# A hybrid decoder step on one core: the sample's state update split anew between ScalarE and VectorE, its loads fetched earlier, and a scan step regrouped

## The chip, the core and the metric

The kernel runs on one core of one Trainium2 chip. Its time is the device time of one execution in microseconds (us). Before the change three runs gave 2443.49, 2448.03 and 2448.24 us, a median of 2448.03.

## What is computed

The reference is one layer of a decoder trunk for a prompt of 1024 tokens and a sample group of 8 tokens, which share all weights. After a modulated RMS norm one input projection feeds attention and a Mamba-2 scan; both are merged, projected, and followed by a second norm and an MLP. The part that the change touches is the scan, with its gate, and the second norm:

```python
def _ssd_mixer(z, xbc, dt_raw, conv_buf, h0, conv_w, conv_b, dt_bias, a_log, d_skip, norm_g):
    xbc, new_buf = _causal_conv(xbc, conv_buf, conv_w, conv_b)
    xs = xbc[..., :D_INNER].reshape(b, L, SSD_HEADS, SSD_HEAD_DIM)
...
    y, h = _ssd(xs, dt, A, Bm, Cm, h0)
    y = y + d_skip.astype(jnp.float32)[:, None] * xs.astype(jnp.float32)
    y = _gated_rmsnorm(y.reshape(b, L, D_INNER).astype(z.dtype), z, norm_g)
    return y, new_buf, h
```

The scan has 32 heads of 64 channels, 8 groups that share their B and C, and a state of 128. For the prompt it goes over 8 chunks of 128 tokens. For a sample, which has one token, it is one update of each state: `h = h * decay + (x * dt) * B`, and then `y = sum(h * C)` over the state.

## The kernel before

**Dense work and side work.** All large products go through the class `Dense`. A job is one block of 128 output features: its weights are loaded by SyncE (L81, tile `wraw`), rounded by ScalarE to a high part (L94, `whi`), and split by GpSimd into the low part (L95, `wlo`). For each of three token chunks (384, 384 and 264 columns) and each of eight slices of the contraction, TensorE makes three matmuls (L140 to L142), 24 for a chunk, into one of 3 PSUM banks called `mm`. Then the job's own evacuation empties the bank. Other work is written as Python generators, the sides. Between two chunks of a dense job a clock advances and the sides are resumed; `yield from rest(n)` lets n such steps pass. They use 5 other PSUM banks, called `ps`.

**Order.** TensorE's order is the order in which the program is written, so the steps of the sides set it. The other engines' orders are made by a scheduler from the dependencies, and they keep it: each takes its instructions one after the other. SyncE issues every DMA, in one queue.

**A group of the scan.** For each of the 8 groups (`gi`) dense jobs compute the gate stream z (L785 tanh on ScalarE, L786 on VectorE) and then four blocks of the stream that goes through the convolution. The first two of these I call x and x', and x.c0 is the first token chunk of x. Their evacuation is L819 on ScalarE, three multiply-adds on VectorE (L823), which free the bank, then a tanh (L832) and one more VectorE step (L833). While they run, three sides work on the group whose convolution is done:

- `decode` updates the sample states. `load(bh)` fetches, for a pair of samples, B and C spread over all partitions (L867, tile `bc`, 256 KB) and for two feature tiles the state (L872, tile `hst`). Each feature tile and sample then has: ScalarE's product of B with x·dt (L887, `tmp`); VectorE's `hst * decay + tmp` (L888); VectorE's sum of `hst * C` (L890). The state is stored (L892), and L893 adds the result to x. A group has 16 updates, the kernel 128.
- `chunks` goes over the 8 chunks. `load(c)` fetches the running sums of the decay (L906, tile `ar`, 256 KB). `prep(c)` transposes x and B and multiplies B with C on TensorE (L917 to L920), empties that bank (L925, L928 and L930 on VectorE, L927 on ScalarE), and turns `ar` into decays (four instructions of L932 and one of L934 on ScalarE, L935 on GpSimd). `state(c)` makes the new state (L941 on TensorE, L944 decay on GpSimd, L947 add on VectorE). `out(c)` makes the output (L956 from the old state, L960 from the chunk; L964, L965 and L967 on VectorE).
- `finish_` multiplies with the gate (L978 on GpSimd), stores (L979), squares (L980 on ScalarE, L981 on VectorE) and sums the squares over the channels (`sums`, on TensorE L284, read by L987).

Some of the groups also have gate jobs among their dense work, whose tanh is stored at L1153.

**The second norm.** Late in the program `norm2(ci)` waits until all eight output projections of a token chunk are done. L284 sums the squares over the channels, a Newton iteration on VectorE takes the reciprocal root, L1407 spreads it over the partitions, and eight feature tiles are normalised (L1410 to L1416) as the input of the MLP's first projection. ScalarE and VectorE square and sum beforehand (L1357, L1358).

## Time and profile before

| | |
|---|---|
| three runs | 2443.49, 2448.03, 2448.24 us; median 2448.03 |
| profiled execution, its own time | 2446.0 us |
| span of its trace | 2444.1 us, mean granted TensorE clock 0.982 |
| busy | TensorE 95%, VectorE 49%, ScalarE 35%, GpSimd 28% |

The profile names engines PE (TensorE), PEld (its weight loads), DVE (VectorE), ACT (ScalarE), POOL (GpSimd) and SP (SyncE). `L888` is a line of the kernel; `hst<-hst,dsel,tmp` is what an instruction writes and reads. An idle time belongs to the engine just before the instruction named, with what ended it behind an arrow. The profiled execution lies 2.0 us below the median of the runs.

### The profile page before, as it was taken

The page shows a single profiled execution, that of the slowest core. Times are in us where ns is not written, and L with a number is a line of the kernel's source. Part 1 is how long each engine was busy: PE and PEld are TensorE (multiplying, and loading weights), DVE is VectorE, ACT ScalarE, POOL GpSimd, SP SyncE. Part 2 cuts the span into 40 slices and gives each one's busy share as a digit, 9 for nine tenths or more (in the row PEclk, how much of TensorE's full clock was granted, in tenths as well). Part 3 has the DMA queues.
Part 4 walks back from the last instruction along what each step waited for, and adds up shares of the span by engine and source line. Part 5 has one row for each costly group of instructions (what it writes and reads, how often), then busy time and mean ns, then how long its engine had stood idle before and what let it go on. Part 6 is the DMA issues. An engine that isn't in the chain of part 4 may idle for free.

```text
span 2444.1 us, 40657 instructions
## 1 busy us (share of the span) xinstructions
PE 2333.1 (95%) x15171; PEld 2227.6 (91%) x15171; DVE 1191.2 (49%) x3224; ACT 861.5 (35%) x2138; POOL 686.8 (28%) x615
## 2 busy tenths in 40 slices
PE   6989999999999989999999899999999999999997
PEld 4868888989888988989999899999999999999997
DVE  3533334575666657476654644546433333333336
ACT  4433433454444444354533331233321221221232
POOL 1102122233333333343443323441222212222230
PEclk8989999999999999999999999999999999999999
DMA  8345434353443434344345532440544444411111
GB/s 304 111 148 158 149 90 101 87 145 107 114 110 98 121 89 118 94 116 123 101 136 153 150 109 87 120 152 22 168 143 149 157 149 152 136 48 44 57 40 70
DMA packets 359588, 288.61 MB, mean 118 GB/s; under 512 B 24030, under 2 KB 350237, under 8 KB 353614
## 3 DMA queue, kind: packets, MB, share of 16 engines
q1 hardware_dynamic: 359390, 286.01, 39.7%
q8 instruction: 120, 1.97, 0.3%
q14 instruction: 78, 0.64, 0.1%
HBM read 243.77 MB, written 88.74 MB: 136 GB/s over the span
## 4 chain that ended last, share of the span: by engine, by line
PE 70%; DMA 12%; DVE 8%; ACT 3%; issue 3%; POOL 3%; SPq 1%; DVEq 0%; ACTq 0%; POOLq 0%
PE mm L140 21%; PE mm L141 21%; PE mm L142 21%; DMA ar<-ac_d 7%; DVE ck L823 2%; ACT ar L932 1%; PE ps L571 1%; DMA wraw<-w_in 1%; POOL wlo L95 1%; DMA bc<-bc_d 1%; DVE hst L888 1%; PE ps L545 1%; POOL ar L935 1%; DVE tmp L890 1%; PE ps L562 1%
## 5 line engine op out<-in xcount | busy, mean ns | idle before, releaser
L140 PE MATMUL mm<-hh,whi 128*128 128x384 f32 (+4 forms) x2808 | 927.1, 330 | 29.8 <-DVE ck L823 27.0
L141 PE MATMUL mm<-hl,whi 128*128 128x384 f32 (+4 forms) x2808 | 902.3, 321 | 0.8 <-DMA xT_d<-xT 0.4
L142 PE MATMUL mm<-hh,wlo 128*128 128x384 f32 (+4 forms) x2808 | 902.1, 321 | 0.0
L95 POOL TENSOR_TENSOR wlo<-wraw,whi 128x512 fp32r<-128x512 f32 (+2 forms) x332 | 425.0, 1285 | 1204.4 <-ACT whi L94 1163.7
L140 PEld LDWEIGHTS mm<-hh,whi 128*128 128x128 f32 (+1 forms) x2808 | 532.5, 190 | 45.0 <-issue 27.7
L141 PEld LDWEIGHTS mm<-hl,whi 128*128 128x128 f32 (+1 forms) x2808 | 531.6, 189 | 5.5 <-DVE hl L417 2.2
L142 PEld LDWEIGHTS mm<-hh,wlo 128*128 128x128 f32 (+1 forms) x2808 | 530.8, 189 | 1.2
L94 ACT CAST whi<-wraw 128x512 fp32r<-128x512 f32 (+2 forms) x332 | 201.4, 610 | 460.0 <-PE mm L141 393.1
L1342 DVE SCALAR_TENSOR_TENSOR acc<-mm,mod,acc 128x384 f32<-128x384 f32 (+1 forms) x216 | 123.5, 572 | 229.4 <-PE mm L142 229.3
L141 PE MATMUL mm<-dl,whi 128*128 128x384 f32 (+1 forms) x696 | 223.3, 321 | 0.0
L142 PE MATMUL mm<-dh,wlo 128*128 128x384 f32 (+1 forms) x696 | 222.3, 319 | 0.0
L140 PE MATMUL mm<-dh,whi 128*128 128x384 f32 (+1 forms) x696 | 222.3, 319 | 0.0
L823 DVE SCALAR_TENSOR_TENSOR ck<-mm,cwT,ck 128x384 f32<-128x384 f32 (+4 forms) x288 | 162.9, 567 | 58.2 <-ACT ck L819 54.2
L1436 DVE TENSOR_TENSOR r<-r 128x384 f32<-128x384 f32 (+1 forms) x96 | 69.5, 724 | 186.0 <-ACT r L1435 186.0
L935 POOL TENSOR_TENSOR ar<-ar,cb 128x512 f32<-128x512 f32 x64 | 84.4, 1323 | 180.4 <-DVE cb L930 170.9
L932 ACT ACTIVATE ar<-ar,acs 128x128 f32<-128x128 f32 x256 | 85.9, 393 | 129.4 <-DMA ar<-ac_d 128.5
L140 PEld LDWEIGHTS mm<-dh,whi 128*128 128x128 f32 x696 | 131.0, 188 | 0.0
L141 PEld LDWEIGHTS mm<-dl,whi 128*128 128x128 f32 x696 | 130.9, 188 | 0.0
L142 PEld LDWEIGHTS mm<-dh,wlo 128*128 128x128 f32 x696 | 130.8, 188 | 0.0
L888 DVE SCALAR_TENSOR_TENSOR hst<-hst,dsel,tmp 128x128 f32<-128x128 f32 x128 | 66.3, 539 | 69.0 <-ACT tmp L887 58.8
L1435 ACT ACTIVATE r<-mm 128x384 f32<-128x384 f32 (+1 forms) x96 | 43.8, 456 | 154.6 <-PE mm L142 154.1
L832 ACT ACTIVATE th<-ck 128x384 f32<-128x384 f32 (+1 forms) x96 | 47.2, 492 | 108.0 <-DVE ck L823 108.0
(358 smaller groups left out, 3371.5 us busy)
## 6 DMA issues: line engine op xcount, KB each, us to landing
wraw<-w_in SPq DMA_DIRECT2D x164, 256.0 KB
kv_g_sample<-cache_kv_g SPq DMA_DIRECT2D x144, 256.0 KB
wada<-w_ada SPq DMA_DIRECT2D x24, 1024.0 KB
ar<-ac_d SPq DMA_DIRECT2D x64, 256.0 KB
wraw<-w_up SPq DMA_DIRECT2D x64, 256.0 KB
wraw<-w_down SPq DMA_DIRECT2D x58, 256.0 KB
hst<-state_ssm SPq DMA_DIRECT2D x64, 128.0 KB
bc<-bc_d SPq DMA_DIRECT2D x32, 256.0 KB
```

Of the source, the lines that this page charges most:

```text
L94: A.copy(hi, raw)
L95: P.tensor_tensor(lo, raw, hi, op=OP.subtract)
L140: T.matmul(ps[:n, :m], wh, a, start=(k == 0), stop=False)
L141: T.matmul(ps[:n, :m], wh, b, start=False, stop=False)
L142: T.matmul(ps[:n, :m], wl, a, start=False, stop=(k == nk - 1))
L823: V.scalar_tensor_tensor(acc[:, o:n], ps[:, x0 + o - d:x0 + n - d], w[k], acc[:, o:n], op0=OP.mult, op1=OP.add)
L832: A.activation(th[:, :nt], acc[:, :nt], AF.Tanh)
L888: V.scalar_tensor_tensor(hst[:, i, :], hst[:, i, :], ds[:, 8 + 2 * bh + i:9 + 2 * bh + i], tmp, op0=OP.mult, op1=OP.add)
L932: A.activation(ar[:, h, :], ar[:, h, :], AF.Relu, bias=acs[:, c, 4 * gi + h:4 * gi + h + 1], scale=-1.0)
L935: P.tensor_tensor(ar, ar, cb[:, None, :].to_broadcast([128, 4, 128]), op=OP.mult)
L1342: V.scalar_tensor_tensor(x[:, t0:t0 + n], ps[:, :n], gate[:, 0:1], x[:, t0:t0 + n], op0=OP.mult, op1=OP.add)
L1436: V.tensor_tensor(r[:, :nt], r[:, :nt], r[:, :nt], op=OP.mult)
```

## The change

Five things change.

1. In `decode`, ScalarE multiplies the state by its decay in place, and VectorE adds B times x·dt to it; before, ScalarE made the product with B and VectorE did the decay and the sum. VectorE's multiply-add now waits for ScalarE's decay, which needs nothing that VectorE makes in that step.
2. `bc` has 3 buffers instead of 2, `hst` 6 instead of 4, and loads are issued for two pairs ahead of the loop and a third in its first step. A step of the side is now one feature tile, with one `rest(1)`, instead of a pair with `rest(2)`.
3. In `chunks`, `prep(c + 3)` and `load(c + 4)` stand in the step of `state(c)`; `out(c)` follows a step later.
4. In `finish_`, the gate's products with their stores and the squares are two steps.
5. In `norm2`, two steps pass before the reciprocal root instead of one.

```diff
--- before.py
+++ after.py
@@ -863,19 +863,20 @@
             def load(bh):
                 if bh > 3:
                     return
-                bc = sd.tile([128, 2, 2, 128], F32, name="bc", tag="bc", bufs=2)
+                bc = sd.tile([128, 2, 2, 128], F32, name="bc", tag="bc", bufs=3)
                 dma(bc, dap(bc_d, gi * 2048 + bh * 256, [[0, 128], [1024, 2], [128, 2], [1, 128]]))
                 hs_ = []
                 for t in range(2):
                     r0 = bh * 2 * 262144 + (4 * gi + 2 * t) * 8192
-                    hst = sd.tile([128, 2, 128], F32, name="hst", tag="hst", bufs=4)
+                    hst = sd.tile([128, 2, 128], F32, name="hst", tag="hst", bufs=6)
                     dma(hst, dap(ws, r0, [[128, 128], [262144, 2], [1, 128]]))
                     hs_.append((r0, hst))
                 got[bh] = bc, hs_
             load(0)
-            yield from rest(2)
+            load(1)
+            yield from rest(3)
             for bh in range(4):
-                load(bh + 1)
+                load(bh + 2)
                 bc, hs_ = got[bh]
                 for t, (r0, hst) in enumerate(hs_):
                     ds = dsel[:, 2 * gi + t, :]
@@ -884,14 +885,14 @@
                     V.tensor_tensor(dx[:, :2], xcol, ds[:, 2 * bh:2 * bh + 2], op=OP.mult)
                     for i in range(2):
                         tmp = sd.tile([128, 128], F32, name="tmp", tag="tmp", bufs=3)
-                        A.mul(tmp, bc[:, 0, i, :], dx[:, i:i + 1])
-                        V.scalar_tensor_tensor(hst[:, i, :], hst[:, i, :], ds[:, 8 + 2 * bh + i:9 + 2 * bh + i],
-                                               tmp, op0=OP.mult, op1=OP.add)
+                        A.mul(hst[:, i, :], hst[:, i, :], ds[:, 8 + 2 * bh + i:9 + 2 * bh + i])
+                        V.scalar_tensor_tensor(hst[:, i, :], bc[:, 0, i, :], dx[:, i:i + 1], hst[:, i, :],
+                                               op0=OP.mult, op1=OP.add)
                         V.tensor_tensor_reduce(tmp, hst[:, i, :], bc[:, 1, i, :], 1.0, 0.0,
                                                OP.mult, OP.add, dx[:, 4 + i:5 + i])
                     dma(dap(wso, r0, [[128, 128], [262144, 2], [1, 128]]), hst)
                     V.scalar_tensor_tensor(xcol, xcol, ds[:, 16:17], dx[:, 4:6], op0=OP.mult, op1=OP.add)
-                yield from rest(2)
+                    yield from rest(1)
             tl['dec'] = 1
 
         A_, S_ = {}, {}
@@ -977,6 +978,8 @@
             for t in range(2):
                 P.tensor_tensor(X[t][ci][:, :nt], X[t][ci][:, :nt], Z[t][ci][:, :nt], op=OP.mult)
                 dma(y_d[2 * gi + t, :, t0:t0 + nt], X[t][ci][:, :nt])
+            yield from rest(1)
+            for t in range(2):
                 A.activation(sq[t][:, :nt], X[t][ci][:, :nt], AF.Square)
             V.tensor_tensor(sq[0][:, :nt], sq[0][:, :nt], sq[1][:, :nt], op=OP.add)
             if nt < 384:
@@ -1002,11 +1005,11 @@
             yield from rest(1)
             for c in range(8):
                 state(c)
-                yield from rest(1)
-                out(c)
                 if c + 3 < 8:
                     prep(c + 3)
                 load(c + 4)
+                yield from rest(1)
+                out(c)
                 tl['c'] = c + 1
                 if c in (2, 5, 7):
                     live[c // 6] -= 2
@@ -1026,7 +1029,7 @@
                 while tl['c'] < min(8, 3 * ci + 3) or tl['nz'] < 6 or (ci == 2 and not tl['dec']):
                     yield 'wait'
                 yield from rest(1)
-                gate(ci)
+                yield from gate(ci)
                 yield from rest(2)
                 sums(ci)
                 yield
@@ -1399,7 +1402,7 @@
             yield 'wait'
         if nt < 384:
             V.memset(ssq[ci][:, nt:], 0.0)
-        yield from rest(1)
+        yield from rest(2)
         r = rstd_cols(ssq[ci], 1.0 / D, EPS, n2)
         yield from rest(1)
         ps = ps_()
```

Since the diff adds lines, L887 becomes L888, L888 becomes L889, L906 becomes L907, L932 becomes L933, L956 becomes L957, L978 becomes L979 and L1407 becomes L1410.

How the order moves is shown at three places. The first is SyncE's queue in group 2 (the third), from the loads of `bc` on. Before:

```order
L867 DMA bc<-bc_d 128x2x256 x2
L81 DMA wraw<-w_in 128x4x128
L892 DMA ssm_sample<-hst 128x2x128
L906 DMA ar<-ac_d 128x4x128
L892 DMA ssm_sample<-hst 128x2x128
L872 DMA hst<-state_ssm 128x2x128
L867 DMA bc<-bc_d 128x2x256
L872 DMA hst<-state_ssm 128x2x128
L892 DMA ssm_sample<-hst 128x2x128 x2
L867 DMA bc<-bc_d 128x2x256
L872 DMA hst<-state_ssm 128x2x128
```

Now:

```order
L867 DMA bc<-bc_d 128x2x256 x3
L81 DMA wraw<-w_in 128x4x128
L893 DMA ssm_sample<-hst 128x2x128 x2
L867 DMA bc<-bc_d 128x2x256
L907 DMA ar<-ac_d 128x4x128
L872 DMA hst<-state_ssm 128x2x128 x2
L893 DMA ssm_sample<-hst 128x2x128 x3
L872 DMA hst<-state_ssm 128x2x128
L893 DMA ssm_sample<-hst 128x2x128
L872 DMA hst<-state_ssm 128x2x128 x3
```

The first `ar` load stood behind one store of sample states; it now stands behind two and behind the fourth `bc` load.

The second place is ScalarE in the same group, around the last `ar` decay ahead of x.c0 (L819). Before:

```order
L887 ACTIVATE tmp<-bc,dx 128x128 x3
L785 ACTIVATE th<-mm 128x264
L94 CAST whi<-wraw 128x512
L887 ACTIVATE tmp<-bc,dx 128x128
L927 COPY bt<-ps 128x128
L932 ACTIVATE ar<-ar,acs 128x128 x4
L887 ACTIVATE tmp<-bc,dx 128x128
L934 ACTIVATE ar<-ar 128x512
L887 ACTIVATE tmp<-bc,dx 128x128
L819 ACTIVATE ck<-mm,vecT,cwT 128x384
L832 ACTIVATE th<-ck 128x384
L819 ACTIVATE ck<-mm,vecT,cwT 128x384
```

Now:

```order
L888 ACTIVATE hst<-hst,dsel 128x128 x3
L94 CAST whi<-wraw 128x512
L785 ACTIVATE th<-mm 128x264
L888 ACTIVATE hst<-hst,dsel 128x128 x5
L933 ACTIVATE ar<-ar,acs 128x128 x4
L935 ACTIVATE ar<-ar 128x512
L819 ACTIVATE ck<-mm,vecT,cwT 128x384
L888 ACTIVATE hst<-hst,dsel 128x128 x3
L928 COPY bt<-ps 128x128
L888 ACTIVATE hst<-hst,dsel 128x128
L832 ACTIVATE th<-ck 128x384
L819 ACTIVATE ck<-mm,vecT,cwT 128x384
```

The two products with B next to the decay of `ar` are gone from the way to x.c0; four decays of states stand right behind its first step, ahead of the tanh (L832) and of x.c1.

The third place is TensorE at the second norm, third token chunk: the spreading of the reciprocal root (L1407, now L1410) and the first matmul on the chunk that is normalised with it (264 columns). The numbers in front are positions in TensorE's order. Before:

```order
8718 L1407 MATMUL ps<-cst,rstd 128x128 x3
8719 L140 MATMUL mm<-hh,whi 128x384
...
8765 L141 MATMUL mm<-hl,whi 128x384
8766 L142 MATMUL mm<-hh,wlo 128x384
8767 L140 MATMUL mm<-hh,whi 128x264
8768 L141 MATMUL mm<-hl,whi 128x264
```

Now:

```order
8742 L1410 MATMUL ps<-cst,rstd 128x128 x3
8743 L140 MATMUL mm<-hh,whi 128x384
...
8765 L141 MATMUL mm<-hl,whi 128x384
8766 L142 MATMUL mm<-hh,wlo 128x384
8767 L140 MATMUL mm<-hh,whi 128x264
8768 L141 MATMUL mm<-hl,whi 128x264
```

Between the two stood 48 dense matmuls; now there are 24.

## Rows read from the trace of the kernel before

**Rows 1.** Page of the profile, part 1: busy time, share of the span, instructions of each engine.

```profile
PE 2333.1 (95%) x15171; PEld 2227.6 (91%) x15171; DVE 1191.2 (49%) x3224; ACT 861.5 (35%) x2138; POOL 686.8 (28%) x615
```

**Rows 2.** Waits of TensorE from 400 to 1260 us: in total, times, longest (us).

```profile
PE mm L140 <- DVE ck L823: 27.0, 17, 2.8
PE ps L956 <- DVE state L947: 11.7, 6, 3.4
...
PE ps L284 <- DVE sq L981: 1.5, 1, 1.5
```

**Rows 3.** Waits of VectorE, then of ScalarE, from 400 to 1260 us.

```profile
DVE hst L888 <- ACT tmp L887: 58.8, 20, 6.3
...
ACT ar L932 <- DMA ar<-ac_d: 128.5, 44, 6.0
```

**Rows 4.** Timeline of SyncE's DMA issues, group 2: start, duration (us), line, what it moves.

```profile
707.30 0.42 SPq L906 DMA_DIRECT2D ar<-ac_d  x1
708.12 0.38 SPq L892 DMA_DIRECT2D ssm_sample<-hst  x1
...
709.69 0.36 SPq L867 DMA_DIRECT2D bc<-bc_d  x1
...
720.66 0.38 SPq L892 DMA_DIRECT2D ssm_sample<-hst  x1
721.09 0.46 SPq L906 DMA_DIRECT2D ar<-ac_d  x1
...
726.38 0.55 SPq L872 DMA_DIRECT2D hst<-state_ssm  x1
```

**Rows 5.** Timeline of ScalarE, group 2; in brackets idle time before it and releaser.

```profile
713.68 1.27 ACT L932 ACTIVATE ar<-ar,acs 128x128 f32<-128x128 f32 x4 [3.26 <-DMA ar<-ac_d]
...
728.78 1.28 ACT L932 ACTIVATE ar<-ar,acs 128x128 f32<-128x128 f32 x4 [4.69 <-DMA ar<-ac_d]
729.96 0.39 ACT L887 ACTIVATE tmp<-bc,dx 128x128 f32<-128x128 f32 x1
...
731.06 0.65 ACT L819 ACTIVATE ck<-mm,vecT,cwT 128x384 f32<-128x384 f32 x1
...
734.43 0.65 ACT L819 ACTIVATE ck<-mm,vecT,cwT 128x384 f32<-128x384 f32 x1
```

**Rows 6.** Timeline of VectorE, group 2.

```profile
730.38 0.35 DVE L888 SCALAR_TENSOR_TENSOR hst<-hst,dsel,tmp 128x128 f32<-128x128 f32 x1 [3.44 <-ACT tmp L887]
...
731.46 0.42 DVE L947 TENSOR_TENSOR state<-ps,state 128x256 f32<-128x256 f32 x1
...
733.30 0.60 DVE L823 SCALAR_TENSOR_TENSOR ck<-mm,cwT,ck 128x383 f32<-128x383 f32 x1
```

**Rows 7.** Timeline of TensorE, group 2.

```profile
732.02 1.19 PE L956 MATMUL ps<-ck,state 128*128 128x128 f32 x4 [3.16 <-DVE state L947]
...
735.18 0.49 PE L140 MATMUL mm<-hh,whi 128*128 128x384 f32 x1
...
751.81 0.41 PE L140 MATMUL mm<-hh,whi 128*128 128x384 f32 x1 [1.66 <-DVE ck L823]
```

**Rows 8.** Timeline of GpSimd, group 2.

```profile
702.27 0.61 POOL L944 TENSOR_TENSOR state<-state,cdk 128x256 f32<-128x256 f32 x1
```

**Rows 9.** Waits of TensorE from 1660 to 1740 us.

```profile
PE ps L284 <- DVE ssq L1358: 3.9, 2, 2.4
```

**Rows 10.** By stretch: busy time of the five queues, then granted clock, DMA share, GB/s.

```profile
530.00:535.30 5.30, 5.30 (x31) 4.75 (x32) 4.96 (x18) 2.58 (x8) 0.00 (x0) 0.68 0.33 65
1697.00:1705.00 8.00, 7.42 (x27) 7.42 (x28) 3.05 (x15) 1.06 (x3) 0.00 (x0) 0.57 0.52 164
```

**Rows 11.** Timeline of VectorE at the second norm's third chunk.

```profile
1717.11 0.42 DVE L1416 TENSOR_TENSOR hl<-ht,hh 128x264 fp32r<-128x264 f32 x1
```

**Rows 12.** Timeline of TensorE there.

```profile
1713.85 0.34 PE L140 MATMUL mm<-hh,whi 128*128 128x384 f32 x1
...
1714.37 0.28 PE L140 MATMUL mm<-hh,whi 128*128 128x264 f32 x1
```

## Prediction

> **What bounds the kernel now.** I read the shares of the engines first. TensorE is busy 95% of the span, VectorE 49%, ScalarE 35% [rows 1]. So nothing that only shortens VectorE or ScalarE pays by itself; what can be won is time in which TensorE stands still, and the list of TensorE's waits between 400 and 1260 us says how much there is. The reader is to see two large entries in it [rows 2]: dense matmuls (L140) that wait 27.0 us for a PSUM bank, released by the convolution sum on VectorE (L823), and 11.7 us in six waits of the output product (L956) for the state (L947). One wait of 1.5 us belongs to the group sums (L284).
>
> Next the waits of the other two engines. VectorE stands 58.8 us before the sample update (L888) for ScalarE's product, in 20 waits. ScalarE stands 128.5 us before the decay of a chunk (L932) for the load of `ar`, in 44 waits [rows 3]. That order matters: both engines take their work in order, so a load that ScalarE waits for also holds back whatever stands behind it there, and VectorE with it.
>
> The timelines of group 2 show how this reaches TensorE. I call the two `ar` loads that SyncE issues at 707.30 and 721.09 us A and B. A stands behind the group's first store of a sample state, B right behind a later one at 720.66 [rows 4]. ScalarE meets A at 713.68 after 3.26 us of waiting and B at 728.78 after 4.69. Only behind B come the last sample products, one at 729.96, and, at 731.06, the first step of x.c0, the first of three dense chunks whose sums already lie in PSUM [rows 5]. VectorE waits 3.44 us for those products, adds the state at 731.46, and starts the last of x.c0's three sums at 733.30 [rows 6]. TensorE waits 3.16 us for that state at 732.02 and goes on with dense work at 735.18; at 751.81 it waits again, 1.66 us, for a bank [rows 7].
>
> So one late load makes both kinds of wait. With sum and duration x.c0's bank is free at 733.30 + 0.60 = 733.90, only 1.28 us before the next dense matmul starts. If the state came in time, that matmul would wait for the bank instead.
>
> **The change part by part.**
>
> *ScalarE only decays.* The number of instructions is the same: one ScalarE product and one VectorE multiply-add for each of 128 updates. VectorE's takes 0.35 us [rows 6], ScalarE's 0.39 us [rows 5], and nothing changes in size. I price the arithmetic at 0. What changes is the wait: the decay needs only the state and can run ahead, so of VectorE's 58.8 us nearly all goes. TensorE sees this only through the state (11.7 us) and the order of stores ahead of A and B.
>
> *Loads of B, C and states three steps ahead.* On SyncE's queue A now has two stores and the fourth `bc` load ahead of it instead of one store. In the trace the second store is issued at 708.12 and A at 707.30; the store after which A may go is the one at 708.12, and the `bc` load, which takes 0.36 us to issue at 709.69, must first have its buffer free, that is the updates of two tiles done. Against 707.30, A's issue moves to about 708.12 + 0.38 + 0.36 = 708.86, so **+1.55 us**. The extra 256 KB lie ahead of it in the transfer too. The nearest rows: A takes 713.68 - 707.30 = 6.4 us from issue to use, B 7.7 us. With four loads of its size around A in the listed order (three of `bc`, one of weights), one more costs between nothing (it would have moved then anyway) and a quarter of 7.7 us, 1.9; I take **+1.3**, nearer the upper end, because both measured times are long. The Trainium skill ("DMA: Bandwidth & Descriptors", section "Anatomy of one DMA — SWDGE (gpsimd) path") fits about 2.0 us plus bytes at 436 GB/s, for another issuing path; by it A would take an estimated 2.6 us and the extra load 0.6, and the sum over six groups would be some 4 us lower. The trace does not agree with the 2.6: it shows 6.4 and 7.7.
>
> *From A to B.* A's use to B's issue is 721.09 - 713.68 = 7.4 us. Of ScalarE's way there four products of 0.39 us, 1.6 us, are gone, and four decays of the last pair come in partly; B gets one store more ahead (0.38 us). I take **-0.9**. Behind B the two products (0.39 each) leave ScalarE ahead of x.c0: **-0.6**, with -0.2 for the transfer of B. GpSimd gets the state's decay ahead of a weight split, 0.61 us [rows 8], which delays the next weight load and `ar` load behind it: **+0.6**. In the groups whose later chunks carry gate jobs, VectorE has less to do between x'.c1 and x'.c2 by its listed order, about **-0.85**, two operations of 0.42 us as L947's.
>
> Sum for a group: 1.55 + 1.3 - 0.9 - 0.2 - 0.6 + 0.6 = +1.7, less 0.85 in groups 1 to 4. That is what x.c0's release and then the gap at 751.81 shift by; the state's waits fall inside it, as said above. Groups 1 to 6: 4 x 0.85 + 2 x 1.7 = **+6.8 us**. Bounds: with A's transfer at +0 and the path to B 2 us shorter instead of 0.9, it is -0.65 a group before the 0.85 (together -7 us); with +1.9 and no saving to B, +3.25 before it (+16 us).
>
> *Group 0* has other waits: 1.5 us for the group sums (L284), seen in the list [rows 2]. The gate in two steps puts the sums a chunk later; that wait goes, and with it the stretch behind it at 0.68 of the clock from 530 to 535.3 [rows 10], 0.32 x 5.3 = 1.7 us of dense work lost. **-3.0**, bounds -4 and 0. For the other groups' gates I take 0: their sums had no wait.
>
> *Preparation beside the state.* The same instructions, a step earlier; L917 to L920 cost TensorE the same wherever they stand. VectorE's three evacuations behind them lie beside dense work: 0. Without that cover they would stand between x.c0's sums, at most 3 x 0.42 = 1.3 us a group by L947's row [rows 6]; the range holds that.
>
> *The second norm's reciprocal root one chunk later.* Before, L284 waits 2 times, 3.9 us in total [rows 9], and the stretch behind the second wait ran at 0.57 of the clock in 8 us [rows 10], some of it at 1.2 and the rest at 2.4 GHz: 0.43 x 8 = 3.4 us lost. Both can go: -7.3. But the broadcast (L1407) of the third token chunk then has 24 matmuls of dense cover less. TensorE starts its first matmul on that chunk at 1714.37, and VectorE begins the chunk's last piece only at 1717.11 [rows 11, 12]: TensorE already takes the pieces as they come. Three dense matmuls start in 0.52 us there (1713.85 to 1714.37), so 24 are 8 x 0.52 = 4.2 us of cover, and what is lost of it is waited. Net -3.1 if the clock stays up, +0.3 if it falls there as it did before. I take **-1.4**.
>
> Sum: 6.8 - 3.0 - 1.4 = +2.4 us on the profiled execution, 2446.0, which lies 2.0 us below the median of 2448.03. Against the median I predict **2450 us**.
>
> **The rivals.** A measurement of this kernel tells about 0.2% (4.9 us) from no change.
>
> *The waits vanish: 2430 us.* If B's landing does not set x.c0's release, because A is early enough once VectorE no longer waits for ScalarE, TensorE loses the 11.7 us, 3.0 in group 0, 3.1 in the norm: -17.8 from 2448.03. If each state wait also lowers the clock, as the wait in group 0 does for 1.7 us, six of them take it to 2420. Against it stands the 1.28 us of slack.
>
> *ScalarE stands behind the states it decays: 2461 us.* Four decays of the next group's updates now stand right behind x.c0's first step on ScalarE, ahead of its tanh and of x.c1, and wait for `hst` loads. The last such load is issued at 726.38 [rows 4]; if it takes as long as B, 7.7 us, it lands at 734.1. The four decays (0.39 each) and the tanh (0.43 until x.c1's step may start) then end at 736.1, where ScalarE took up x.c1 at 734.43 before [rows 5]: 1.7 us late, and VectorE's sums for the second bank with it. It decides from the point where the load lands after 734.43 - 2.0 = 732.4. Six groups make +10.2; with the forecast's +2.4, 2448.03 + 12.6 = 2460.6. The Trainium skill ("PSUM — Partial Sum Buffer", section "Engine vs sequencer instructions") says that ScalarE's and VectorE's queues are strictly first in, first out. The trace agrees: the product at 729.96 comes only behind B's decay [rows 5].
>
> *Nothing moves.* If the scheduler's new order leaves A and B where they were, only the norm and group 0 remain: 2448.0 - 4.4 = 2443.6. The listed order speaks against it; it changes at both places.
>
> **How the numbers follow.** Forecast (gains and losses cancel): 0.40, its own range 2444 to 2457. The waits vanish: 0.28. ScalarE behind the states, or A and B at their upper bound (+16 - 4.4 on the median, 2460): 0.24. Nothing moves: 0.08. Faster than 2443.1: all of the second case and half of the last, 0.32. Slower than 2452.9: the third case and a fifth of the forecast, 0.32. The rest, 0.36, within 0.2%. The range 2429 to 2464 leaves out the ends of the second and third case, at most 0.2 together.
>
> **What would show it.** Right: VectorE's wait before L889 for ScalarE below 10 us in place of 58.8; TensorE's wait for the state below 3 us; its wait for L823 not below the old 27.0 but near 35; A's use at about 716 relative to the same point of group 2. In the norm: no wait of L284, and a new wait of about 4 us on the third chunk's matmuls. Wrong: if TensorE's wait for L823 also falls, the bank was not bound by A and B; if ScalarE shows waits before L888 for `hst` loads, the third case holds. If both kinds of wait are as predicted and the time still moves by over 5 us, the clock did it.

## The result and the profile after

The changed kernel took 2463.36 us (median of 4 runs, 2460.96 to 2464.15) beside 2448.14 us (4 runs, 2443.49 to 2450.83) of the kernel before: a ratio of 1.0057, 95% interval 1.0036 to 1.0079. It is 15 us slower. The forecast was 2450 us, no change that can be measured; the measured time lies inside the range of 2429 to 2464, near its upper end.

The profiled execution spans 2461.1 us, 17.0 more than before. Part 1 of the page, and then TensorE's, VectorE's and ScalarE's waits between 400 and 1280 us (in total, times, longest), answer to [rows 1 to 3]:

```profile
PE 2341.1 (95%) x15171; PEld 2236.2 (91%) x15171; DVE 1184.8 (48%) x3224; ACT 859.6 (35%) x2138; POOL 685.0 (28%) x615
```

```profile
PE mm L140 <- DVE ck L823: 44.8, 20, 4.6
```

```profile
DVE ck L823 <- ACT ck L819: 126.7, 35, 11.4
...
DVE hst L889 <- DMA bc<-bc_d: 30.3, 8, 4.2
```

```profile
ACT ar L933 <- DMA ar<-ac_d: 184.9, 41, 10.4
```

The wait for the state, 11.7 us before, is not in TensorE's list any more, and VectorE no longer waits for ScalarE's product: before L889 it waits for `bc`. Both are what the change was to do. But the wait for a bank went from 27.0 to 44.8 us, and ScalarE now stands 184.9 us before the decay of a chunk, where it stood 128.5. With fewer instructions that depend on VectorE, ScalarE comes to a load earlier and stands there longer; in the mean of groups 2 to 6 it starts x.c0 no earlier (24.6 us after the group's start, 24.5 before).

Two windows over the scan, of before and then of after, which begin and end with the same dense chunks, show what most of the 17 us consist of. The columns are the window, its length, then busy time and instructions of TensorE, its weight loads, VectorE, ScalarE and GpSimd, the granted clock, and the share and GB/s of the DMAs:

```profile
481.55:1346.00 864.45, 817.76 (x5456) 784.46 (x5454) 538.12 (x1551) 387.37 (x1001) 321.04 (x293) 0.99 0.44 116
```

```profile
482.89:1359.95 877.06, 824.06 (x5456) 793.25 (x5454) 534.18 (x1552) 384.83 (x1001) 320.41 (x293) 0.97 0.44 115
```

The window is 12.6 us longer. TensorE's idle time in it went from 864.45 - 817.76 = 46.7 to 877.06 - 824.06 = 53.0 us, so 6.3 us are more waiting. The other 6.3 us are busy time: as many matmuls (5456) took longer, at a mean granted clock of 0.97 in place of 0.99 (part of it at 1.2, the rest at 2.4 GHz). Of the remaining 4.4 us, 1.3 lie ahead of the window and 3.1 behind it, these nearly all in the second norm.

**Group 2 after the change.** SyncE, ScalarE and VectorE around A, B and x.c0, for [rows 4 to 6]. First SyncE:

```profile
708.77 1.67 SPq L893 DMA_DIRECT2D ssm_sample<-hst  x2
710.53 0.42 SPq L867 DMA_DIRECT2D bc<-bc_d  x1
711.05 0.44 SPq L907 DMA_DIRECT2D ar<-ac_d  x1
...
723.61 0.47 SPq L907 DMA_DIRECT2D ar<-ac_d  x1
```

The order is the listed one: two stores, the fourth load of `bc`, then A at 711.05, and B at 723.61. ScalarE:

```profile
716.32 1.28 ACT L933 ACTIVATE ar<-ar,acs 128x128 f32<-128x128 f32 x4 [8.80 <-DMA ar<-ac_d]
...
729.70 1.28 ACT L933 ACTIVATE ar<-ar,acs 128x128 f32<-128x128 f32 x4 [6.05 <-DMA ar<-ac_d]
...
731.54 0.66 ACT L819 ACTIVATE ck<-mm,vecT,cwT 128x384 f32<-128x384 f32 x1
732.61 1.00 ACT L888 ACTIVATE hst<-hst,dsel 128x128 f32<-128x128 f32 x3 [0.41 <-issue]
...
734.84 0.53 ACT L832 ACTIVATE th<-ck 128x384 f32<-128x384 f32 x1 [0.77 <-DVE ck L823]
735.27 0.66 ACT L819 ACTIVATE ck<-mm,vecT,cwT 128x384 f32<-128x384 f32 x1
```

A is met at 716.32 and B at 729.70. x.c0's first step follows at 731.54, 1.84 us behind B where it was 2.28. Three decays of states stand at 732.61, and x.c1 follows x.c0 after 3.73 us where it was 3.37 [rows 5]. The decays are not what x.c1 waits for: ScalarE stands 0.77 us before the tanh (L832) for VectorE's last sum, and x.c1 comes right behind the tanh. VectorE, after the change and then, for the same place, before it:

```profile
732.23 0.62 DVE L823 SCALAR_TENSOR_TENSOR ck<-mm,cwT,ck 128x381 f32<-128x381 f32 x1 [4.62 <-ACT ck L819]
732.76 0.41 DVE L926 TENSOR_TENSOR xd<-ps,dtk 128x256 f32<-128x256 f32 x1
733.10 0.61 DVE L823 SCALAR_TENSOR_TENSOR ck<-mm,cwT,ck 128x382 f32<-128x382 f32 x1
733.79 0.42 DVE L929 TENSOR_TENSOR xw<-ps,dcy 128x256 f32<-128x256 f32 x1
734.14 0.60 DVE L823 SCALAR_TENSOR_TENSOR ck<-mm,cwT,ck 128x383 f32<-128x383 f32 x1
```

```profile
731.79 0.60 DVE L823 SCALAR_TENSOR_TENSOR ck<-mm,cwT,ck 128x381 f32<-128x381 f32 x1
732.32 0.40 DVE L890 CUSTOM_DVE_ANT_0 tmp<-hst,bc 128x128 f32<-128x128 f32 x1
...
733.18 0.20 DVE L893 SCALAR_TENSOR_TENSOR ck<-ck,dsel,dx 128x2 f32<-128x2 f32 x1
733.30 0.60 DVE L823 SCALAR_TENSOR_TENSOR ck<-mm,cwT,ck 128x383 f32<-128x383 f32 x1
```

Between the three sums of x.c0 (L823) stand two evacuations of the preparation, L926 and L929; from the start of the first sum to the end of the last are 734.74 - 732.23 = 2.5 us. Before, two shorter steps of the sample update stood there (L890, L893), and it was 733.90 - 731.79 = 2.1 us. In group 6 of the changed kernel the gap is wider. ScalarE, then VectorE there:

```profile
1163.03 0.98 ACT L888 ACTIVATE hst<-hst,dsel 128x128 f32<-128x128 f32 x3 [0.72 <-DVE xd L926]
1163.92 0.24 ACT L928 COPY bt<-ps 128x128 f32<-128x128 f32 x1
```

```profile
1164.20 0.42 DVE L929 TENSOR_TENSOR xw<-ps,dcy 128x256 f32<-128x256 f32 x1 [0.91 <-ACT bt L928]
```

Three decays stand on ScalarE ahead of the copy of `bt`, VectorE waits 0.91 us for that copy between two sums, and the three sums take 3.3 us. TensorE in group 2 [rows 7]:

```profile
734.89 0.41 PE L140 MATMUL mm<-hh,whi 128*128 128x384 f32 x1 [2.22 <-DVE ck L823]
...
753.36 0.66 PE L140 MATMUL mm<-hh,whi 128*128 128x384 f32 x1 [1.97 <-DVE ck L823]
```

TensorE waits 2.22 us where the state stalled it before, now for the bank of x.c0, and 1.97 us at the second place. From x.c0's first step on ScalarE to the end of that second wait are 753.36 - 731.54 = 21.8 us; before, 751.81 - 731.06 = 20.8 [rows 5, 7]. Group 2 shows the places but not the loss: from its start to x.c0's first step it takes 24.1 us in place of 25.7, so that by the end of the second wait it has lost nothing in all. Group 6 lost most, with 25.6 and 22.8 us in place of 23.4 and 20.6.

The granted clock of this place, by windows of before and then of after (columns as above), and the matmuls of after on either side of its fall:

```profile
732.00:735.20 3.20, 3.18 (x18) 2.65 (x18) 2.55 (x8) 1.08 (x2) 0.57 (x1) 0.50 0.46 124
```

```profile
736.20:739.60 3.40, 3.40 (x12) 3.40 (x11) 3.40 (x9) 0.61 (x2) 0.41 (x2) 0.51 0.00 0
```

```profile
736.01 0.33 PE L140 MATMUL mm<-hh,whi 128*128 128x384 f32 x1
...
736.75 0.52 PE L140 MATMUL mm<-hh,whi 128*128 128x384 f32 x1
```

Both times the clock fell from 2.4 to 1.2 GHz at or behind a wait of TensorE. Before, the low stretch lay over the output products behind the wait for the state; after, it begins 1.3 us behind the end of the wait for the bank and lies over dense matmuls, which take 0.52 us each where they took 0.33. By its place, then, the low clock follows a wait for the bank as it followed one for the state.

### The profile page after: what moved, and what is told of

It reads as the page before. It is cut to its first block, busy times and chain, and to the rows that moved or that the text cites. A ratio compares the mean times of both kernels' runs of the same rounds, so it can differ in the third digit from the quotient of the medians.

```text
span 2461.1 us, 40677 instructions
## 1 busy us (share of the span) xinstructions
PE 2341.1 (95%) x15171; PEld 2236.2 (91%) x15171; DVE 1184.8 (48%) x3224; ACT 859.6 (35%) x2138; POOL 685.0 (28%) x615
## 3 DMA queue, kind: packets, MB, share of 16 engines
q8 instruction: 120, 1.97, 0.3%
## 4 chain that ended last, share of the span: by engine, by line
PE 67%; DMA 11%; DVE 10%; issue 4%; ACT 3%; POOL 3%; SPq 1%; POOLq 0%; DVEq 0%; ACTq 0%
PE mm L140 21%; PE mm L141 20%; PE mm L142 20%; DMA ar<-ac_d 5%; DVE ck L823 2%; PE ps L571 1%; ACT ar L933 1%; POOL wlo L95 1%; DMA qb<-qkv_d 1%; DMA ssm_sample<-hst 1%; DMA bc<-bc_d 1%; DVE hst L889 1%; DMA wraw<-w_in 1%; PE ps L545 1%; DVE ck L833 1%
## 5 line engine op out<-in xcount | busy, mean ns | idle before, releaser
L140 PE MATMUL mm<-hh,whi 128*128 128x384 f32 (+4 forms) x2808 | 930.6, 331 | 49.9 <-DVE ck L823 44.8
L1345 DVE SCALAR_TENSOR_TENSOR acc<-mm,mod,acc 128x384 f32<-128x384 f32 (+1 forms) x216 | 123.4, 573 | 229.6 <-PE mm L142 229.5
L823 DVE SCALAR_TENSOR_TENSOR ck<-mm,cwT,ck 128x384 f32<-128x384 f32 (+4 forms) x288 | 162.7, 566 | 130.5 <-ACT ck L819 126.7
L933 ACT ACTIVATE ar<-ar,acs 128x128 f32<-128x128 f32 x256 | 84.9, 392 | 196.3 <-DMA ar<-ac_d 184.9
L833 DVE SCALAR_TENSOR_TENSOR ck<-th,ck 128x384 f32<-128x384 f32 (+1 forms) x96 | 74.1, 772 | 36.1 <-ACT th L832 34.3
L945 POOL TENSOR_TENSOR state<-state,cdk 128x256 f32<-128x256 f32 x56 | 34.5, 616 | 176.9 <-DVE state L948 176.9
```

Source lines behind the costliest of these rows:

```text
L140: T.matmul(ps[:n, :m], wh, a, start=(k == 0), stop=False)
L823: V.scalar_tensor_tensor(acc[:, o:n], ps[:, x0 + o - d:x0 + n - d], w[k], acc[:, o:n], op0=OP.mult, op1=OP.add)
L833: V.scalar_tensor_tensor(acc[:, :nt], th[:, :nt], 1.0, acc[:, :nt], op0=OP.add, op1=OP.mult)
L933: A.activation(ar[:, h, :], ar[:, h, :], AF.Relu, bias=acs[:, c, 4 * gi + h:4 * gi + h + 1], scale=-1.0)
L1345: V.scalar_tensor_tensor(x[:, t0:t0 + n], ps[:, :n], gate[:, 0:1], x[:, t0:t0 + n], op0=OP.mult, op1=OP.add)
```

## Experiments

All runs below stand beside runs of the kernel before on the same chip; each ratio is to these. To compare the traces I cut groups 2 to 6, which repeat one another, at two points: from the group's start to x.c0's first step on ScalarE, and from there to the end of TensorE's second bank wait. The start is the dense chunk that began at 705.33 us in group 2 before and at 707.44 after. The means over the five groups, in us, one profiled execution each:

| kernel | ratio to before, 95% interval | start to x.c0 | x.c0 to end of second wait |
|---|---|---|---|
| before | 1 | 24.5 | 20.6 |
| the change | 1.0057 (1.0036 to 1.0079) | 24.6 | 22.6 |
| e1, without the preparation's move | 1.0070 (1.0057 to 1.0082) | 25.1 | 20.8 |
| e2, the preparation's move alone | 1.0072 (1.0059 to 1.0085) | 26.0 | 22.0 |
| e3, the sample part alone | 1.0041 (1.0028 to 1.0055) | 25.5 | 20.8 |
| e7, its arithmetic alone | 1.0066 (1.0053 to 1.0079) | 25.2 | 21.5 |
| e8, its loads and steps alone | 1.0009 (0.9994 to 1.0025) | 24.8 | 20.5 |
| e4, the gate alone | 1.0005 (0.9992 to 1.0018) | 24.4 | 20.5 |
| e5, before with 8 chunk buffers | 0.9983 (0.9969 to 0.9996) | 24.2 | 20.3 |
| e6, the change with 8 chunk buffers | 1.0110 (1.0092 to 1.0128) | 27.4 | 21.4 |
| e12, e5 and e8 | 0.9979 (0.9966 to 0.9992) | 24.1 | 20.0 |

The two stretches are some 45 of the 94 to 110 us of a group, and the rest of a group can give back what they lose. From the start of group 2 to the dense chunk that began at 1222.27 us before, behind group 6, the traces are longer than that of before by 8.8 us (the change), 2.9 (e1), 8.3 (e2), 6.5 (e3), 3.6 (e7) and 1.7 (e8); e4's is 2.9 shorter. Since neither e4's nor e8's time can be told from that of before, a few us between two traces are no finding.

### The change without one part, and single parts

My first theory was that the preparation beside the state costs most; the rival was the first chunk load, late behind the sample's stores and loads.

**e1** puts these lines back in the changed kernel:

```diff
                 state(c)
-                if c + 3 < 8:
-                    prep(c + 3)
-                load(c + 4)
                 yield from rest(1)
                 out(c)
+                if c + 3 < 8:
+                    prep(c + 3)
+                load(c + 4)
```

> The change without one part: preparation and chunk load stand again in the step after the state, as before the change; all else as changed. Theory (preparation beside the state): its three evacuations on VectorE (0.42 + 0.42 + 0.28 us) stand between the convolution sums of x.c0, and GpSimd's state decay (0.61 us) ahead of a weight split, some 1.5 to 2 us a group in groups 1 to 7; without it 10 to 13 us of the 15.2 come back, about 2451 us. Rival (the first late chunk load, issued 0.9 to 2.5 us later behind the states' stores and loads): it stays late here, so 2459 or more. Second rival (the norm): 2463 less nothing.

Measured: 2461.13 us beside 2444.19, ratio 1.0070. Nothing came back. As an account of the whole loss the theory is wrong, although its place is right: without the move the stretch behind x.c0 shrank from 22.6 to 20.8 us, and groups 2 to 6 as a whole by 8.8 - 2.9 = 5.9 us. In exchange the stretch ahead of x.c0 grew by 0.5 us, and groups 0 and 1 took 6.4 us longer than before (3.2 each), where with the move they took 1.2 longer (-0.9 and +2.1).

**e2** is the kernel before with that edit alone, the other way round:

```diff
                 state(c)
-                yield from rest(1)
-                out(c)
                 if c + 3 < 8:
                     prep(c + 3)
                 load(c + 4)
+                yield from rest(1)
+                out(c)
```

> The kernel before with one part of the change alone: preparation and chunk load in the state's step. Theory (preparation beside the state): 8 to 12 us slower than before, about 2458 us, with the wait for the state (11.7 us before) mostly kept or turned into waits for the bank. Rival (late chunk load): no change, 2448 within 3 us.

Measured: 2461.63 us beside 2444.19, ratio 1.0072. The move alone costs 17 us, more than the 8 to 12 expected and as much as the whole change. TensorE's wait for the state is gone and its wait for the bank has nearly doubled:

```profile
PE mm L140 <- DVE ck L823: 50.1, 22, 4.8
```

The stretch behind x.c0 grew by 1.4 us and the one ahead of it by 1.5, and group 0 alone lost 5.3 us. So the rival "no change" fell too, and the edit does not depend on the sample part to do harm.

**e3** is the kernel before with the sample part, which is e7's and e8's edits below together:

```diff
-                bc = sd.tile([128, 2, 2, 128], F32, name="bc", tag="bc", bufs=2)
+                bc = sd.tile([128, 2, 2, 128], F32, name="bc", tag="bc", bufs=3)
...
-                        A.mul(tmp, bc[:, 0, i, :], dx[:, i:i + 1])
...
+                        A.mul(hst[:, i, :], hst[:, i, :], ds[:, 8 + 2 * bh + i:9 + 2 * bh + i])
...
```

> The kernel before with the sample update's part alone: ScalarE on the decay, a feature tile a step, loads further ahead. Theory (preparation beside the state): within 4 us of before, 2444 to 2452; TensorE's wait for the state is gone, its wait for the bank (27.0 us) grows by some 5 us. Rival (late chunk load): 6 us or more slower, 2454 and up, with the waits for the bank at 40 us or more.

Measured: 2454.26 us beside 2444.19, ratio 1.0041: 10 us slower, as the rival had it. The wait for the bank is about as long as the rival said:

```profile
PE mm L140 <- DVE ck L823: 39.8, 20, 3.6
```

**e4** is the kernel before with the gate in two steps.

```diff
+            yield from rest(1)
+            for t in range(2):
                 A.activation(sq[t][:, :nt], X[t][ci][:, :nt], AF.Square)
...
-                gate(ci)
+                yield from gate(ci)
```

> The kernel before with the gate's part alone: products and squares in two steps. All theories: group 0's wait for the sums goes; 1 to 3 us faster, 2445 to 2447, which may be too little to tell from no change. Rival (the squares, a step later, come in the way of VectorE's convolution sums in the groups that follow): 2 us or more slower.

Measured: 2446.77 us beside 2444.19, ratio 1.0005, interval 0.9992 to 1.0018. It cannot be told from no change.

### Which half of the sample part: arithmetic or loads

**e7** changes only the arithmetic in the kernel before:

```diff
-                        A.mul(tmp, bc[:, 0, i, :], dx[:, i:i + 1])
-                        V.scalar_tensor_tensor(hst[:, i, :], hst[:, i, :], ds[:, 8 + 2 * bh + i:9 + 2 * bh + i],
-                                               tmp, op0=OP.mult, op1=OP.add)
+                        A.mul(hst[:, i, :], hst[:, i, :], ds[:, 8 + 2 * bh + i:9 + 2 * bh + i])
+                        V.scalar_tensor_tensor(hst[:, i, :], bc[:, 0, i, :], dx[:, i:i + 1], hst[:, i, :],
+                                               op0=OP.mult, op1=OP.add)
```

> The kernel before with the sample update's arithmetic alone: ScalarE decays the state, VectorE adds B times x dt; buffers, loads and steps as before. If the 10 us that the whole sample part cost come from the order of its loads and stores (the first chunk load behind the second store and the fourth load of B and C), this is within 3 us of before or faster, with that load at its old place. If they come from the decays on ScalarE, 6 us or more slower.

Measured: 2459.22 us beside 2444.79, ratio 1.0066. The decays alone cost 14 us. The timeline of ScalarE in group 4 of this kernel shows one place:

```profile
963.99 0.65 ACT L819 ACTIVATE ck<-mm,vecT,cwT 128x384 f32<-128x384 f32 x1
...
966.69 0.52 ACT L832 ACTIVATE th<-ck 128x384 f32<-128x384 f32 x1 [1.46 <-DVE ck L823]
967.12 1.27 ACT L887 ACTIVATE hst<-hst,dsel 128x128 f32<-128x128 f32 x4
968.28 0.65 ACT L819 ACTIVATE ck<-mm,vecT,cwT 128x384 f32<-128x384 f32 x1
```

Four decays stand between x.c0's tanh (L832) and x.c1's first step. x.c1 follows x.c0 after 968.28 - 963.99 = 4.29 us, where it was 3.37 before [rows 5]; VectorE's sums for the second bank start that much later. None of these decays waits for anything. Groups 0 and 1 lost 7.0 and 3.2 us, groups 2 to 6 together 3.6.

**e8** has the other half, loads further ahead and a feature tile a step, with the arithmetic of before:

```diff
-                bc = sd.tile([128, 2, 2, 128], F32, name="bc", tag="bc", bufs=2)
+                bc = sd.tile([128, 2, 2, 128], F32, name="bc", tag="bc", bufs=3)
...
-                    hst = sd.tile([128, 2, 128], F32, name="hst", tag="hst", bufs=4)
+                    hst = sd.tile([128, 2, 128], F32, name="hst", tag="hst", bufs=6)
...
-            yield from rest(2)
+            load(1)
+            yield from rest(3)
...
-                load(bh + 1)
+                load(bh + 2)
...
-                yield from rest(2)
+                    yield from rest(1)
```

> The kernel before with the sample part's loads and steps alone: more buffers, loads further ahead, a feature tile a step; ScalarE still makes the product with B. Theory of late loads (two stores and a further load of B and C ahead of the first chunk load): that load issued 1 to 2 us later and 4 to 8 us slower. Theory of decays (they hold ScalarE where they wait for states, in group 0 and between the first steps of x.c0 and x.c1): without them within 3 us of before.

Measured: 2446.72 us beside 2445.05, ratio 1.0009, interval 0.9994 to 1.0025. So the loads and steps cost nothing by themselves. SyncE's queue in group 2 shows that they don't make the first chunk load late either:

```profile
708.18 0.38 SPq L893 DMA_DIRECT2D ssm_sample<-hst  x1
708.65 0.42 SPq L907 DMA_DIRECT2D ar<-ac_d  x1
...
711.65 0.41 SPq L867 DMA_DIRECT2D bc<-bc_d  x1
```

A stands behind one store and ahead of the fourth load of `bc`, as it did without the edit. So e8 tests what the edit costs, not what a late load costs. In the kernels whose A stands behind two stores (the change, e1, e2, e3, e7, e6, e10) it is issued 2.9 to 5.6 us after the group's start in the mean of groups 2 to 6; where it stands behind one (before, e4, e5, e8, e9, e11, e12), 2.0 to 2.3 us. Of the kernels with 3 banks, the first are the slower ones and the second are not. Whether the late load is a cause of their loss ahead of x.c0 or comes with it, no run tells: none moves A alone. TensorE waits less for banks and still waits for the state, since that is behind ScalarE's product:

```profile
PE mm L140 <- DVE ck L823: 20.7, 13, 2.7
PE ps L957 <- DVE state L948: 13.3, 6, 3.0
```

### Taking the wait itself away

If ScalarE's wait for a chunk load sets the bank, loads that come earlier should help. **e5** does that to the kernel before, and **e6** to the changed one:

```diff
-            ar = D_[c] = sd.tile([128, 4, 128], F32, name="ar", tag="ar", bufs=5)
+            ar = D_[c] = sd.tile([128, 4, 128], F32, name="ar", tag="ar", bufs=8)
...
-            for c in range(4):
+            for c in range(min(8, 7)):
                 load(c)
...
-                load(c + 4)
+                load(c + 7)
```

> The kernel before, with 8 instead of 5 buffers for the chunk decays (ar) and their loads three chunks further ahead; nothing else. Theory (ScalarE's wait for a late chunk load sets when x.c0's bank comes free): ScalarE's 128.5 us before L932 fall below 30, TensorE's waits for bank and state (27.0 + 11.7) to about 20, and the time by 10 to 18 us, to about 2433. Rival (VectorE's order of evacuations sets it, the loads are only near): TensorE's waits within 8 us of before, the time within 5 us.

> The changed kernel with the same 8 buffers and loads further ahead. Theory (late loads, plus preparation between the convolution sums): the late-load part goes, 10 to 18 us faster than the changed kernel, about 2448; what preparation and norm cost stays, so it is 8 us or more slower than the kernel before with the same buffers. Rival (late loads alone): as fast as that kernel, the norm's 3 us apart.

Measured: e5 2438.48 us beside 2444.79, ratio 0.9983; e6 2473.30 us beside the same, ratio 1.0110. e5 is 6 us faster, about half of what was expected, and e6 is slower still than the change, where it was to be 10 to 18 us faster. TensorE's and ScalarE's waits in e5, then ScalarE's in e6:

```profile
PE mm L140 <- DVE ck L823: 23.7, 13, 4.2
PE ps L956 <- ACT ck L819: 6.9, 5, 2.6
```

```profile
ACT ar L932 <- DMA ar<-ac_d: 108.7, 40, 5.7
```

```profile
ACT ar L933 <- DMA ar<-ac_d: 124.6, 38, 8.4
```

ScalarE's wait fell from 128.5 to 108.7 us in e5, far from the 30 expected, and from 184.9 to 124.6 in e6. The trace of e6 tells why: each chunk's decay on ScalarE was moved ahead with its load. In group 4 the load issued at 944.30 us, among the sample's stores, is for the first chunk of the next group. ScalarE met it at 951.23, ahead of x.c0, although the output product that uses it (L961) runs at 1050.80. So this was no clean test of earlier loads. The kernel before has the same order in small: B's decay at 728.78 stands ahead of x.c0, and the output product that needs it (L960) runs at 762.46. A version whose decay stands behind x.c0's first step has not been tried.

### A fourth bank

The last test of the bank gives dense sums 4 of the 8 PSUM banks and the side work 4: **e9** on the kernel before, **e10** on the changed one, **e11** on e5.

```diff
-        return psum.tile([128, 512], F32, name="mm", tag="mm", bufs=3)
+        return psum.tile([128, 512], F32, name="mm", tag="mm", bufs=4)
...
-        return psum.tile([128, 512], F32, name="ps", tag="ps", bufs=5)
+        return psum.tile([128, 512], F32, name="ps", tag="ps", bufs=4)
```

> The kernel before with 4 PSUM banks for dense sums instead of 3, and 4 for the side work instead of 5. Theory (the bank of x.c0 is what both kernels run into, so TensorE gets one more chunk, some 4 us, of slack): TensorE's wait for L823 falls from 27.0 to under 10 us; its wait for the state (11.7) stays; 8 to 14 us faster than before. Rival (side work needs its fifth bank): new waits of side products for banks, no faster or slower.

> The changed kernel with the same 4 and 4 banks. Theory (bank of x.c0): its 44.8 us for L823 fall under 15 and, the wait for the state being gone, it is faster than the kernel before with 4 banks but for the norm's 3 us: some 25 to 30 us faster than the changed kernel, about 2436, and the time at the lower clock in the scan falls from 47.8 us below 30. Rival (the chain of loads, ScalarE and VectorE is itself too long for a group, whatever the banks): the wait only moves, less than 8 us gained.

> A version from the experiments: the kernel before with 8 chunk buffers, loaded further ahead, and 4 and 4 banks. If the gains of the two add up: 6 from the loads and 8 to 14 from the banks, 14 to 20 us faster than before, about 2428. If they remove the same wait: no faster than the better of the two alone.

Measured: e9 2471.37 us (ratio 1.0105), e10 2489.69 us (1.0181), e11 2469.16 us (1.0092), beside 2445.05 us. All are slower, as the rival of e9 allowed, and e9 loses it ahead of the scan: the dense chunk that began at 511.90 us before begins at 545.24. That the stages there need the fifth bank is likely but was not tested apart. Within the scan the test still says something. TensorE's longest waits in e10:

```profile
PE ps L957 <- DVE cb L931: 27.1, 7, 5.9
PE ps L799 <- ACT last L830: 14.1, 6, 3.0
```

In e9 the wait for L823 is gone, and the scan from that chunk on is 6 us shorter than before. In e10 the wait for L823 falls to 0.9 us, but 27.1 us of waiting for the preparation's `cb` and 14.1 for ScalarE's copy (L830) stand in its place. There the scan is 14 us longer than in e9 and 4 us shorter than in the change: as the rival said, less than 8 us gained. The time at the low clock, which was to fall below 30 us, is 44 us there. That the chain of ScalarE and VectorE is too long for its group, and the bank only the place where TensorE meets it, fits this but is not shown by it, since the side work has a bank less too.

### A version that beats both

**e12** is e5 with the loads and steps of e8 (both diffs above), and none of the other edits.

> A version from the experiments: the kernel before with the sample part's loads and steps (8 us less wait for banks in the trace, no measured time) and the 8 chunk buffers loaded further ahead (6 us faster); ScalarE's product, preparation, gate and norm as before. If the two gains add up: 6 to 10 us faster than before, with TensorE's waits for bank and state under 25 us. If the further steps only move the waits: as fast as the chunk buffers alone, 6 us, or less.

Measured: 2439.96 us (12 runs, 2434.66 to 2444.50) beside 2444.66, ratio 0.9979, interval 0.9966 to 0.9992. It is 5 us faster than before, no better than e5 within the intervals; the two gains don't add up. Both stretches of the group are the shortest in the table, and TensorE waits 29.7 us in the two places where it waited 38.7; under 25 was expected if the gains added up:

```profile
PE mm L140 <- DVE ck L823: 23.4, 16, 4.2
PE ps L957 <- DVE state L948: 6.3, 6, 2.4
```

## Why the prediction was right, and which of its steps were wrong

The measured time lies in the range with 0.6 us to spare. That is luck: the forecast was no change that can be measured, 15 us were lost, and the terms of the sum do not give them. The range reached so far up for cases that did not occur, decays that wait for late states, and A and B at their upper bound.

**What bounds the kernel: right.** The forecast said that a state in time would only move TensorE's wait to the bank of x.c0. That is what happened: 11.7 us of waiting for the state went to nothing and 17.8 came on top at the bank, 44.8 in all where about 35 was forecast. VectorE's 58.8 us for ScalarE's product went to nothing as well, without a gain. The first rival, waits that vanish, was excluded for the reason given.

**A and B: right in place, the transfer term wrong.** All figures are means of groups 2 to 6. A was put 1.55 us later and was issued 3.7 us after the group's start where it was 2.3, 1.4 later, with the second store and the fourth `bc` load ahead of it as forecast. The transfer term of +1.3 is what failed: from issue to use A took 5.5 us where it took 5.9, and in group 2 716.32 - 711.05 = 5.3 where it was 6.4. The way from A's use to B's issue grew by 0.3 (-0.9 forecast), B's transfer shrank by 0.7 (-0.2), and behind B 0.6 were saved (-0.6). So x.c0 starts at 24.6 us of the group where it started at 24.5, not 1.1 later. The estimate of 2.6 us, worked out in the prediction from the fit of the Trainium skill ("DMA: Bandwidth & Descriptors", section "Anatomy of one DMA — SWDGE (gpsimd) path") for another issuing path, agrees with neither 5.3 nor 6.4.

**Preparation beside the state: the step that failed.** It was priced at 0, "covered by dense work", with 1.3 us a group if the cover was gone. The cover was gone: TensorE waited for the bank of x.c0 at 734.89, right behind the last sum's end at 734.74, so the evacuations between these sums were on the path. From x.c0 to the end of the second wait a group took 22.6 us in place of 20.6. Setting this one part against its absence, it is 22.6 - 20.8 = 1.8 us with the rest of the change and 22.0 - 20.6 = 1.4 without. The rows give the place of most of it. From the first to the last of x.c0's sums a group took 2.8 us in the changed kernel and 1.9 in e1, 2.3 in e2 and 2.1 before; and from the first step of x' to the end of the second wait it took 3.15 us in the three kernels that have the move and 3 banks (the change, e2, e6) and 2.75 in all others with 3 banks. In groups 2 to 6 the move is most of what the change lost (5.9 of 8.8 us). That the whole part brought nothing when it was undone (e1) comes from groups 0 and 1, which lost in its absence what the others gained; why they did is open.

**ScalarE only decays: priced at 0, costs 14 us alone.** The second rival named the place, decays between x.c0's and x.c1's first steps, and a time of 2461 us, nearer than the forecast's. Its mechanism, decays that wait for late states, is not what the rows show: in group 2 after the change only 0.41 us is idle ahead of them, and in e7 four of them run with no wait. In e7 their running time delays x.c1 by 0.9 us. In the changed kernel it doesn't: x.c1 waits there for VectorE's sums, and the decays hold back another thing, the copy of `bt` (0.91 us in group 6). Where most of e7's loss in groups 0 and 1 arises was not tested.

**Group 0**: -3.0 forecast; it and the stretch ahead of it gave -0.5 - 0.9 = -1.4 us in the trace. L284's wait went. That it is the gate's doing is not shown: with the gate alone (e4) the same two pieces are together 1.6 us longer than before. **Gate**: 0 forecast for the other groups, and no change measured (e4).

**The second norm: wrong sign.** Forecast -1.4. From the dense chunk that began at 1663.39 us before to 20 chunks later, the profiled executions take 87.0, 88.6, 86.9 and 88.6 us with the edit (the change, e1, e6, e10) and 82.6 to 85.6 in the others; before has 84.2. No run has this edit alone. TensorE's waits there after the change, for [rows 9]:

```profile
PE ps L284 <- DVE ssq L1361: 3.0, 2, 1.5
PE mm L141 <- DVE hl L1419: 1.2, 3, 0.5
PE mm L141 <- POOL hl L1419: 0.9, 1, 0.9
```

L284's wait was to vanish and is 3.0 us, from 3.9. The new wait for the normalised pieces is there, as forecast, with 2.1 us where about 4 was forecast. Why L284 still waits, VectorE's timeline shows:

```profile
1711.91 0.56 DVE L1413 TENSOR_TENSOR ht<-acc,ps 128x384 f32<-128x384 f32 x1 [0.74 <-POOL hl L1419]
...
1713.12 0.48 DVE L1345 SCALAR_TENSOR_TENSOR acc<-mm,mod,acc 128x256 f32<-128x256 f32 x1
...
1715.36 0.43 DVE L1361 TENSOR_TENSOR ssq<-ssq,tg 128x264 f32<-128x264 f32 x1 [0.49 <-ACT tg L1360]
```

Normalisation of the second chunk also moved a step later, so that VectorE works on it (L1413, itself waiting for GpSimd) up to the moment when the last residual (L1345) and squares (L1361) of the third chunk are due. The forecast moved the reader of the sum and not the work ahead of its writer.

**The clock** was no term of the sum outside group 0 and the norm. It should have been: of 12.6 us in the scan 6.3 were more busy time at a lower clock; TensorE stood at 1.2 GHz for 50 us of that window, for 24 before. Since TensorE's waits were only to change their place, the forecast took the clock behind them as unchanged. They became longer ones, up to 4.6 us where 3.4 was the longest at the state and 2.8 at a bank. That the longer waits brought the clock down is argued from their place, not shown by an experiment. Nor does the time at the low clock tell the loss by itself: e8, whose time can't be told from that of before, has 41 us of it between the same dense chunks.

## What to carry to other kernels

Where a wait is short of a second limit by about a microsecond, as the state was by 1.28 us, work out what the second limit does with every instruction that the change adds ahead of it, and don't price an instruction at 0 because the engine it runs on is half idle. Here an instruction that waited for nothing was not free either: the decays of states ran ahead of a step on which the freeing of a bank depended, x.c1's first step in e7 and the copy of `bt` in the changed kernel. Try the parts of a change alone before they are judged together; of the five here two cost 14 and 17 us each alone, two nothing that can be measured, the fifth (the norm) was not run alone, and none was shown to gain.

## What was not expected of the hardware

Two edits that cost 17 and 10 us alone (e2, e3) cost 15 us together, the norm's 3 us included. Each of them alone already puts A behind a second store; that they lengthen one chain, for whose end TensorE waits once, is the likely reason, and not shown. Buffers that let a load run three chunks ahead moved much of the load's wait instead of removing it, 124.6 us of ScalarE's time with 8 buffers where 5 gave 184.9, part of it for loads that were not needed before the next group. And TensorE's busy time in the scan grew by 6.3 us with the same number of matmuls, so that a wait's price is not read from the list of waits alone.
